# Reordering the start of a chunked linear recurrence: when input tiles are normalised, and which unit's levels go first

## The chip, the core and the metric

The kernel runs on one NeuronCore of one Trainium2 chip. The metric is the device time of one execution in microseconds (us), the median over several runs. The engines are named as in the profile: PE (matmuls; PEld is its weight loads), DVE (VectorE), ACT (ScalarE), POOL (GpSimd) and SP (the queue from which the DMAs are issued). Each engine works through its own queue in order.

## What is computed

One layer of a hybrid mixer over 2048 tokens of 1024 channels: RMS norm, one input projection that is split among three branches, an output projection, a second RMS norm and a residual. The branch that matters here is the first, a gated linear recurrence in four heads of 64 by 64 state:

```python
def step(S, inp):
    qi, ki, vi, gi = inp
    b = jnp.cumsum(gi, axis=2)
    decay = jnp.exp(jnp.where(causal, b_t - b_s, 0.0)) * causal_f
    attn = jnp.einsum('bhtd,bhsd,bhtsd->bhts', qi, ki, decay)
    o = einsum(attn, vi) + einsum(qi * jnp.exp(b), S)
    S = jnp.exp(b_last)[..., None] * S + einsum(ki * jnp.exp(b_last - b), vi)
    return S, o
```

The other two branches, a trailing-window mean and a causal attention with forget gates in eight heads, come after it in the program and are not touched.

## The kernel before, in words

**Input tiles.** The 2048 tokens are 16 tiles of 128, tile 0 to tile 15. `x_parts` (lines 205 to 223) prepares one tile in steps: a load of 512 KB (`xt`, SP), the square with its row sum (`xh`, `ss`, ACT L213), a small sum (DVE L214), a power (POOL L217), the scaled high half (`xh`, ACT L218), the low half (`xl`, DVE L220), and two transposing DMAs into `hTh` and `hTl` (SP L221, L223). Loads go into two `xt` buffers, so a tile's load can be issued when the tile two before it has been read for the last time, by its L220.

**Units.** The recurrence is worked in eight units, four groups `g` of 512 tokens by two channel blocks `ct`: unit 0 is (g 0, ct 0), unit 1 is (0, 1), unit 2 is (1, 0). A name such as `b_1_0` carries g and ct. A unit has three parts:

- features, `hgrn_f` (line 247) and `hgrn_q`: a projection on PE (`pf`, `pq`), then a chain over ACT, DVE and POOL: `E` and `z` (L254 to L257), `sg` (L260), `E` again (L265 to L269), the running sum `b` (L271), `nb` (L274), the factors `Kd` and `Qd` (L281 to L283, L308), `khat`, `qhat` (L286 to L289, L309), `el` (L291), and `qs` from the second projection (L301 to L307);
- levels, `hgrn_unit` (line 315): first matmuls `pd` with the mask `at` (L327, L329) and the transposed keys `khT` (PE L333, ACT L335); then for six block sizes h = 64, 32, 16, 8, 4, 2 a tile `X` (POOL L348, L349, ACT L350), two halves of `Z` (DVE L355), the matmul `pl` (PE L359) and a masked copy into `at` (DVE L363). After the second level the state moves on: `pu` from `khT` (PE L368) and eight updates of `S` (DVE L378). After the fourth, `po` is begun from those states (PE L383);
- the end: `po` is finished (PE L391), squared (ACT L394), summed (DVE L396, L397), raised to a power (POOL L398), scaled to `ma` (DVE L400) and stored.

**What sets the order.** The Python code is the program order. A scheduler then lays the instructions of every engine out, with program order as the priority. An edit of the code's order therefore moves instructions on all engines. In the first part of the program (`ordered`) the given order is kept.

**Around the change.** Tiles 0 to 5 are prepared for the first projections. Before unit 0's levels, tiles 6 and 7 are prepared and tiles 8 and 9 loaded ahead. From then on `feed` (line 596) yields three steps a tile, and every level of a unit takes one step (`next(xfeed, None)`, line 385), so that tiles 8 and 9 are prepared behind unit 0's six levels, 10 and 11 behind unit 1's, and so on. For each unit the loop then works through the next unit's features, the end of the unit before, and this unit's levels, with other projections (`pi`, `pk`) between the levels. Unit 0 has an order of its own (`if n == 0`).

Of the kernel before, what the change touches and what calls it, by code (L numbers as in the profile page):

```python
# [23 lines left out]
NT = T // P  # L24
# [19 lines left out]
GCPRE = 8  # L44
RATE = 0.45
POOL_LV = (64, 32, 16, 8, 4, 2)
LOGP = math.log(256.0)
NEG = -1e30

# [5 lines left out]
def kernel(  # L55
# [144 lines left out]
    def x_dma(xpool, t, tag="xt"):  # L200
        xt = (xpool if tag == "xt" else ap).tile([P, D], F32, tag=tag, name=f"xt{t}", bufs=2)
        sp(nc.sync.dma_start(xt, xf[t * P:(t + 1) * P, :]))
        xts[t] = xt
# [21 lines left out]
    def x_load(xpool, t, tag="xt"):  # L225
        for _ in x_parts(xpool, t, tag):
            pass
# [20 lines left out]
    def hgrn_f(g, ct, wf, bank=None):  # L248
        u = f"_{g}_{ct}"
        pf = (bank or pj)(f"pf{u}")  # L250
        proj_cm(pf, wf, ct * P, g)
        yield
        z, E = tmp(f"z{u}"), tmp(f"E{u}")
        S.activation(E, pf, AF.Abs, bias=0.0, scale=INV)  # L254
        S.activation(z, pf, AF.Copy, bias=0.0, scale=INV)
        S.activation(E, E, AF.Exp, bias=0.0, scale=-1.0)
        S.activation(E, E, AF.Ln, bias=1.0, scale=1.0)  # L257
        sg = tmp(f"sg{u}")

        V.scalar_tensor_tensor(sg, z, 0.0, E, op0=ALU.min, op1=ALU.subtract)  # L260
        E1 = V if g == 0 else G
        E1.tensor_tensor(z, sg, z, op=ALU.subtract)
        lk = lbt[:, 8 + ct:9 + ct]

        V.tensor_scalar(E, sg, -43.0, None, op0=ALU.max)  # L265
        S.activation(E, E, AF.Exp, bias=0.0, scale=-1.0)
        S.activation(E, E, AF.Ln, bias=lbt[:, 4 + ct:5 + ct], scale=lbt[:, 2 + ct:3 + ct])
        V.tensor_tensor(E, E, sg, op=ALU.add)
        V.tensor_scalar(E, E, lbt[:, 6 + ct:7 + ct], None, op0=ALU.max)  # L269
        b = t512("b", f"b{u}")  # L270
        V.tensor_tensor_scan(b, d0, E, initial=0.0, op0=ALU.mult, op1=ALU.add)  # L271

        nb = t512("nb", f"nb{u}")
        V.scalar_tensor_tensor(nb, z, lk, b, op0=ALU.add, op1=ALU.subtract)  # L274

        lfo = sg
        E1.tensor_tensor(lfo.rearrange("p (n two) -> p n two", two=2),
                        E.rearrange("p (n two) -> p n two", two=2),
                        odd.unsqueeze(1).to_broadcast([P, GT // 2, 2]), op=ALU.mult)
        q_d, k_d = t512("Qd", f"Qd{u}"), t512("Kd", f"Kd{u}")  # L280
        E1.tensor_tensor(k_d, z, lfo, op=ALU.subtract)  # L281
        S.activation(k_d, k_d, AF.Exp, bias=lk, scale=1.0)
        S.activation(q_d, lfo, AF.Exp, bias=0.0, scale=1.0)  # L283
        kk = t512("khat", f"khat{u}")
        bt = b.rearrange("p (n t) -> p n t", t=P)
        G.tensor_tensor(kk.rearrange("p (n t) -> p n t", t=P), bt[:, :, P - 1:P].to_broadcast([P, 4, P]), nb.rearrange("p (n t) -> p n t", t=P), op=ALU.add)  # L286
        S.activation(kk, kk, AF.Exp, bias=0.0, scale=1.0)
        e = t512("qhat", f"qhat{u}")
        S.activation(e, b, AF.Exp, bias=0.0, scale=1.0)  # L289
        el = ap.tile([P, 4], F32, tag="el", name=f"el{u}", bufs=2)  # L290
        V.tensor_copy(el, e.rearrange("p (n t) -> p n t", t=P)[:, :, P - 1])  # L291
        feats[(g, ct)] = dict(nb=nb, b=b, qd=q_d, kd=k_d, kk=kk, qh=e, el=el)
# [19 lines left out]
    def run(steps):  # L312
        for _ in steps:
            pass

    def hgrn_unit(g, ct, va):
        f = feats.pop((g, ct))
        nb, b, qs = f["nb"], f["b"], f["qs"]
# [19 lines left out]
        for li, h in enumerate(LEVELS):  # L338
            X = t512("X", f"X{u}_{h}", 4)
            Z = Zs[zc[0] % NZ]  # L340
            zc[0] += 1
            bv = b.rearrange("p (n two h) -> p n two h", two=2, h=h)
            nbv = nb.rearrange("p (n two h) -> p n two h", two=2, h=h)
            Xv = X.rearrange("p (n two h) -> p n two h", two=2, h=h)
            n = GT // (2 * h)
            mid = bv[:, :, 0, h - 1:h].to_broadcast([P, n, h])
            E1 = G if h in POOL_LV else V
            E1.tensor_tensor(Xv[:, :, 1, :], bv[:, :, 1, :], mid, op=ALU.subtract)  # L348
            E1.tensor_tensor(Xv[:, :, 0, :], mid, nbv[:, :, 0, :], op=ALU.add)  # L349
            S.activation(X, X, AF.Exp, bias=0.0, scale=1.0)  # L350
            qv = qs.rearrange("p (t n two h) -> p t n two h", t=4, two=2, h=h)
            X5 = X.rearrange("p (t n two h) -> p t n two h", t=4, two=2, h=h)
            for hh in range(2):
                r = slice(64 * hh, 64 * hh + 64)
                V.tensor_tensor(Z[r, :, hh, :].rearrange("p t (n h) -> p t n h", h=h), X5[r, :, :, 1, :], qv[r, :, :, 1, :], op=ALU.mult)  # L355
            pl = pm(f"pl{u}_{h}")
            plv = pl.rearrange("p (t u c) -> p t u c", t=4, u=2)
            for tt in range(4):
                PE.matmul(plv[:, tt].rearrange("p u c -> p (u c)"), X[:, tt * P:(tt + 1) * P], Z[:, tt].rearrange("p u c -> p (u c)"),  # L359
                          start=tt == 0, stop=tt == 3, skip_group_check=True)  # L360
            n2 = 64 // h
            dst = at.rearrange("p t u (n two h) -> p (t u) n two h", two=2, h=h)[:, :, :, 1, :]
            V.copy_predicated(dst, masks[h].rearrange("p (n h) -> p n h", h=h).unsqueeze(1).to_broadcast([P, 8, n2, h]),  # L363
                              pl.rearrange("p (u n h) -> p u n h", u=8, h=h))
            if li == 1:
                pu = pm(f"pu{u}")
                for tt in range(4):
                    PE.matmul(pu[:, tt * P:(tt + 1) * P], khT[:, tt * P:(tt + 1) * P], va[:, tt, ct * P:(ct + 1) * P],  # L368
                              start=tt == 0, stop=tt == 3, skip_group_check=True)
                olds = []  # L370
                for tt in range(4):
                    old = Sst[ct][Scur[ct] % NS]
                    Scur[ct] += 1
                    new = Sst[ct][Scur[ct] % NS]
                    olds.append(old)
                    for hh in range(2):
                        r = slice(64 * hh, 64 * hh + 64)
                        V.scalar_tensor_tensor(new[r, r], old[r, r], f["el"][r, tt:tt + 1],  # L378
                                               pu[r, tt * P + 64 * hh:tt * P + 64 * hh + 64], op0=ALU.mult, op1=ALU.add)
            if li == 3:  # L380
                po = pm(f"po{u}")
                for tt in range(4):
                    PE.matmul(po[:, tt * P:(tt + 1) * P], f["qh"][:, tt * P:(tt + 1) * P], olds[tt], start=tt == 0, stop=False,  # L383
                              skip_group_check=True)
            next(xfeed, None)
            if li % 2 == 1:
                yield "L"
        for tt in range(4):
# [69 lines left out]
    xpool = xstk.enter_context(tc.tile_pool(name="xpool", bufs=2, side="right", reuse_waits="tile"))  # L458
# [32 lines left out]
    wf, load, halves = w_parts([(FA, 256)], "f")  # L491
# [41 lines left out]
    wq = load_w([(QA, 256)], "q")  # L533
# [11 lines left out]
    for h in LEVELS:  # L545
# [4 lines left out]
                        fill=0, base=0, channel_multiplier=1)  # L550
        G.affine_select(out=m, in_=m, pattern=[[2 * h, nb], [0, h]], compare_op=ALU.is_ge,
                        fill=0, base=h - 1, channel_multiplier=-1)
# [35 lines left out]

    run(hgrn_q(0, 0, wq))
    wk0 = load_w([(KCOL, 256)], "k0", pool=gwp)  # L590
    x_load(xpool, 6)
    x_dma(xpool, 8)
    x_load(xpool, 7)
    x_dma(xpool, 9)

    def feed():

        for t in range(8, NT):
            parts = x_parts(xpool, t)
            for k in range(3):  # L600
                next(parts)
                if k < 2:
                    yield
            next(parts, None)
            if t + 2 < NT:
                x_dma(xpool, t + 2)
            yield

    xfeed = feed()
    prev = None  # L610
    kq = None
    for n, (g, ct) in enumerate(units):
# [24 lines left out]
        if n == 0:  # L637
            fs, qs = hgrn_f(0, 1, wf, pm), hgrn_q(0, 1, wq)
            next(fs)
            next(qs)  # L640
            toks[1] = new_tokens(1)
            tok_i(4, wi, toks[1])
            tok_i(5, wi, toks[1])
            next(gen)
            next(gen)
            run(fs)
            run(qs)
            fill(0)
            next(gen)
            fill(1)  # L650
            fill(2)
            fill(3)
            next(gen)
            prev = gen
            continue
# [547 lines left out]
```

## Time and profile before

| | us |
|---|---|
| median of 3 runs | 1248.82 (1247.8 to 1250.89) |
| the profiled execution's own time | 1248.18 |
| its span, first to last instruction | 1246.4 |
| PE busy | 1170.5 (94% of the span) |
| DVE busy | 812.2 (65%) |
| ACT busy | 609.5 (49%) |
| POOL busy | 403.7 (32%) |

How to read it: the busy shares are over the whole span. The recurrence with its features takes about the first fifth; what follows it are projections, attention and the output projection. The clock of PE is given as the share of its full speed that was granted, 1.00 for 2.4 GHz and 0.5 for 1.2 GHz; a stretch between the two has had both.

### The profile page before, as it was taken

Reading aid. Unit: us, or ns where it says so; the run is one execution under the profiler, and the core shown is the slowest. Engines: PE = TensorE matmul, PEld = TensorE weight load, DVE = VectorE, ACT = ScalarE, POOL = GpSimd, SP = SyncE. Lnnn points to the kernel's source line nnn. Section 1 sums busy time; section 2 is a strip of 40 time slices with the busy share of each in tenths; the row PEclk is TensorE's granted clock in tenths of the full one; section 3 lists DMA queues with packets and bytes.
Section 4 is the critical chain, followed back from the end, with each engine's and each line's share of the span. In section 5 each row is a group of like instructions: output and inputs, shape, how many; then the busy total and the mean of one; then the engine's idle time right before and its main releaser. Section 6 shows DMA issues by size and latency. Waiting matters only on the chain.

```text
span 1246.4 us, 25487 instructions
## 1 busy us (share of the span) xinstructions
PE 1170.5 (94%) x9949; PEld 749.9 (60%) x9949; DVE 812.2 (65%) x1736; ACT 609.5 (49%) x1176; POOL 403.7 (32%) x500
## 2 busy tenths in 40 slices
PE   5877999999999999999999999999989899999998
PEld 3445667655644588884447767755555555555544
DVE  5787878887433243214364799788788888888522
ACT  5756444553121222212122677667767676777611
POOL 2645555553130020002230223234334343434400
PEclk9988999999999999999999999999999999999999
DMA  9646100113175232101112343285223222321263
GB/s 226 184 115 170 44 17 18 52 35 93 43 183 142 71 107 71 35 2 43 26 51 70 89 140 110 69 178 127 67 64 85 68 78 79 65 51 38 80 162 104
DMA packets 168137, 107.56 MB, mean 86 GB/s; under 512 B 95824, under 2 KB 159568, under 8 KB 168016
## 3 DMA queue, kind: packets, MB, share of 16 engines
q1 hardware_dynamic: 166976, 105.92, 32.2%
q8 instruction: 78, 1.28, 0.4%
q14 instruction: 43, 0.35, 0.1%
q10 hardware_dynamic: 1040, 0.00, 0.0%
HBM read 59.62 MB, written 31.59 MB: 73 GB/s over the span
## 4 chain that ended last, share of the span: by engine, by line
PE 62%; DVE 19%; ACT 6%; issue 5%; POOL 4%; DMA 4%; SPq 0%; POOLq 0%; DVEq 0%; ACTq 0%
PE y L1078 11%; PE pq L183 7%; PE pv L194 6%; PE pgc L194 5%; PE pu L183 3%; PE st L1009 3%; PE st L1010 3%; PE pgb L183 3%; PE pk L183 3%; DVE pl L1024 3%; PE mx L973 3%; DVE M L979 3%; PE o L1034 2%; PE o L1035 2%; PE pf L183 2%
## 5 line engine op out<-in xcount | busy, mean ns | idle before, releaser
L1019 ACT ACTIVATE pf<-st,biasg 128x512 f32<-128x512 f32 (+1 forms) x320 | 199.6, 625 | 93.9 <-PE st L1010 53.2
L194 PEld LDWEIGHTS <-hTh 128*128 128x128 f16 x1536 | 151.0, 99 | 44.3 <-DMA hTh<-xh 16.1
L1024 DVE TENSOR_TENSOR pl<-pf,ph 128x512 f16<-128x512 f32 (+1 forms) x213 | 139.9, 658 | 42.4 <-POOL ph L1021 24.8
L1024 POOL TENSOR_TENSOR pl<-pf,ph 128x512 f16<-128x512 f32 (+2 forms) x107 | 114.2, 1067 | 147.7 <-ACT ph L1023 137.6
L979 DVE TENSOR_REDUCE M<-mx 128x1 f32<-128x512 f32 x192 | 129.2, 682 | 9.4 <-PE mx L973 8.5
L1023 ACT ACTIVATE ph<-st,biasg 128x512 f16<-128x512 f32 (+2 forms) x213 | 131.4, 617 | 2.1 <-PE o L1036 2.1
L1034 PE MATMUL o<-Vt,ph 128*128 128x65 f16 x1088 | 129.7, 193 | 2.8 <-DVE oc L1048 2.4
L1035 PE MATMUL o<-Vt,ph 128*128 128x64 f16 x1088 | 130.2, 195 | 0.0
L1036 PE MATMUL o<-Vt,pl 128*128 128x65 f16 x1088 | 129.2, 192 | 0.0
L1021 POOL TENSOR_SCALAR ph<-pf 128x512 f16<-128x512 f32 (+1 forms) x107 | 66.0, 617 | 192.4 <-ACT pf L1019 130.8
L1034 PEld LDWEIGHTS <-ph 128*128 128x128 f16 x1088 | 102.6, 96 | 34.5 <-issue 5.5
L1009 PE MATMUL st<-QQ,K 128*128 128x512 f16 (+1 forms) x320 | 111.5, 349 | 5.6 <-ACT ph L1023 5.0
L1035 PEld LDWEIGHTS <-ph 128*128 128x128 f16 x1088 | 101.8, 97 | 24.5 <-issue 1.1
L1036 PEld LDWEIGHTS <-pl 128*128 128x128 f16 x1088 | 102.3, 99 | 0.4
L1078 PE MATMUL y<-woh,mh 128*128 128x512 f16 (+2 forms) x264 | 98.2, 373 | 0.0
L1078 PE MATMUL y<-woh,ml 128*128 128x512 f16 (+2 forms) x264 | 98.0, 373 | 0.0
L1078 PE MATMUL y<-wol,mh 128*128 128x512 f16 (+2 forms) x264 | 98.0, 373 | 0.0
L973 PE MATMUL mx<-KA,QM 68*128 68x512 f16 (+1 forms) x224 | 79.5, 358 | 5.7 <-DVE M L979 4.1
L194 PEld LDWEIGHTS <-hTl 128*128 128x128 f16 x768 | 75.5, 98 | 9.9
L1010 PE MATMUL st<-QB,KA 68*128 68x512 f16 x224 | 80.1, 358 | 0.0
L1078 PEld LDWEIGHTS <-mh 128*128 128x128 f16 x528 | 49.4, 98 | 50.4 <-issue 0.7
L976 DVE CUSTOM_DVE_ANT_0 mx<-mx,negq 128x128 f32<-128x128 f32 (+3 forms) x128 | 62.3, 492 | 12.0 <-PE mx L973 11.5
(327 smaller groups left out, 2691.1 us busy)
## 6 DMA issues: line engine op xcount, KB each, us to landing
xt<-in_x_dram SPq DMA_DIRECT2D x16, 512.0 KB, 4.4
xr<-in_x_dram SPq DMA_DIRECT2D x16, 512.0 KB, 4.5
out_dram<-yt SPq DMA_DIRECT2D x15, 512.0 KB, 3.1
QQ<-qh_d SPq DMA_DIRECT2D x64, 64.0 KB, 2.3
wo<-in_w_out_dram SPq DMA_DIRECT2D x16, 256.0 KB, 3.0
gc_d<-gtc SPq DMA_DIRECT2D x32, 128.0 KB, 2.0
gtl<-gc_d SPq DMA_DIRECT2D x16, 256.0 KB, 2.9
wst_q<-in_w_in_dram SPq DMA_DIRECT2D x12, 256.0 KB, 2.9
```

The costliest lines, as they stand in the source:

```text
L183: PE.matmul(ps, a[:, k, c0:c0 + P], b[:, k, :], start=i == 0, stop=i == 3 * KC - 1)
L194: PE.matmul(ps, a[:, k, :], b[:, k, c0:c0 + n], start=i == 0, stop=i == 3 * KC - 1)
L979: V.tensor_reduce(dst, mx[:, :w], op=ALU.max, axis=AX.X)
L1009: PE.matmul(st[:, off:], K2[c][:, h, jj * P:(jj + 1) * P], QQs[i][:, off:], start=True, stop=False)
L1010: PE.matmul(st[:, off:], KA[c][:68, h, jj * P:(jj + 1) * P], QBs[i][:68, off:], start=False, stop=not diag)
L1019: S.activation(pf[:, off:], st[:, off:], AF.Exp, bias=bias, scale=0.125)
L1023: S.activation(ph[:, off:], st[:, off:], AF.Exp, bias=bias, scale=0.125)
L1024: (G if k == 1 else V).tensor_tensor(pl[:, off:], pf[:, off:], ph[:, off:], op=ALU.subtract)
L1034: PE.matmul(pov[:, qi, :], ph[:, qs], Vt[:, j, h, 0:65], start=(j == 0 and qi == 0), stop=False, skip_group_check=True)
L1035: PE.matmul(pov[:, qi, 0:64], ph[:, qs], Vt[:, j, h, 65:129], start=False, stop=False, skip_group_check=True)
L1036: PE.matmul(pov[:, qi, :], pl[:, qs], Vt[:, j, h, 0:65], start=False, stop=(j == 4 * g + qi), skip_group_check=True)
L1078: PE.matmul(py, a[:, k, :], b[:, k, cs], start=i == 0, stop=i == 3 * KC - 1)
```

## The change

Three edits. First, tiles 6 and 7 are no longer prepared before unit 0: only their loads are issued there, and `feed` begins with tile 6. A table FEED says how many steps each level takes: in unit 0 one, one, one, two, two, two, in unit 1 the other way round, in units 2 and 3 one each, none later. So tiles 6 to 8 belong to unit 0, 9 to 11 to unit 1, and from tile 12 on the units are those of before. Second, the first step of `hgrn_f` now includes the two ACT instructions that empty the projection's PSUM bank. Third, unit 1 (`n == 1`) gets an order of its own: only the two projections of unit 2's features, with the emptying of the first, go ahead of unit 1's levels; the rest of `hgrn_f` comes behind the first two levels and the rest of `hgrn_q` behind the next two. No arithmetic is changed, and the number of instructions is the same.

```diff
+FEED = ((1, 1, 1, 2, 2, 2), (2, 2, 2, 1, 1, 1), (1,) * 6, (1,) * 6) + ((0,) * 6,) * 4
...
         proj_cm(pf, wf, ct * P, g)
-        yield
         z, E = tmp(f"z{u}"), tmp(f"E{u}")
         S.activation(E, pf, AF.Abs, bias=0.0, scale=INV)
         S.activation(z, pf, AF.Copy, bias=0.0, scale=INV)
+        yield
...
-            next(xfeed, None)
+            for _ in range(FEED[2 * g + ct][li]):
+                next(xfeed)
...
-    x_load(xpool, 6)
-    x_dma(xpool, 8)
-    x_load(xpool, 7)
-    x_dma(xpool, 9)
+    x_dma(xpool, 6)
+    x_dma(xpool, 7)
...
-        for t in range(8, NT):
+        for t in range(6, NT):
...
+        if n == 1:
+
+            fs, qs = hgrn_f(nxt[0], nxt[1], wf), hgrn_q(nxt[0], nxt[1], wq)
+            next(fs)
+            next(prev)
+            next(qs)
+            next(gen)
+            fill(0)
+            fill(1)
+            next(gen)
+            run(fs)
+            fill(2)
+            next(gen)
+            run(qs)
             fill(3)
             next(gen)
             prev = gen
+            continue
```

What the scheduler makes of it is seen in the built order of each engine. The line numbers of the changed kernel are two or three higher than those of before (L213 is L215, L220 is L222, L271 is L273, L335 is L337, L355 is L357). Three places follow.

The first place is ACT's queue ahead of `khT`, the transposed keys of unit 0. Before:

```order
L266 ACTIVATE E_0_1_774<-E_0_1_774 128x512
L304 ACTIVATE th_0_1_804<-th_0_1_804 128x512
L213 ACTIVATE xh7_593,ss7_592<-xt7_590 128x1024
L213 ACTIVATE xh8_742,ss8_741<-xt8_588 128x1024
L218 ACTIVATE xh7_593<-xt7_590,ss7_592 128x1024
L239 ACTIVATE va1_654<-pi5_682 128x256
L240 ACTIVATE fcs_72<-pi5_682 128x8
L335 ACTIVATE khT_0_0_727<-pk_0_0_722 128x512
```

Now:

```order
L220 ACTIVATE xh7_855<-xt7_578,ss7_854 128x1024
L268 ACTIVATE E_0_1_606<-E_0_1_606 128x512
L306 ACTIVATE th_0_1_780<-th_0_1_780 128x512
L241 ACTIVATE va1_634<-pi5_662 128x256
L242 ACTIVATE fcs_72<-pi5_662 128x8
L269 ACTIVATE E_0_1_606<-E_0_1_606,lbt_324 128x512
L307 ACTIVATE th_0_1_780<-th_0_1_780 128x512
L215 ACTIVATE xh8_910,ss8_909<-xt8_835 128x1024
L337 ACTIVATE khT_0_0_707<-pk_0_0_702 128x512
```

The squares of tile 7 and its high half have moved forward. The square of tile 8 still stands ahead of `khT`, but tile 8's load is now issued after tile 6 is done instead of ahead of all.

The second place is DVE from the gate's running sum `b` of unit 2 to the second half of `Z` of unit 1's level 8, for which PE waits. Before:

```order
L274 SCALAR_TENSOR_TENSOR nb_1_0_986<-z_1_0_970,lbt_324,b_1_0_984 128x512
L291 COPY el_1_0_999<-qhat_1_0_997 128x4
L214 TENSOR_SCALAR ss13_1527<-ss13_1527 128x1
L307 TENSOR_TENSOR qs_1_0_1048<-th_1_0_1043,pq_1_0_1018 128x512
L220 SCALAR_TENSOR_TENSOR xl13_1529<-xt13_1238,ss13_1527,xh13_1528 128x1024
L214 TENSOR_SCALAR ss14_1760<-ss14_1760 128x1
L363 COPY_PREDICATED at_0_1_1052<-m64_397,pl_0_1_64_1132 128x8x64
L355 TENSOR_TENSOR Z0_454<-X_0_1_8_1187,qs_0_1_809 64x4x64
L363 COPY_PREDICATED at_0_1_1052<-m32_401,pl_0_1_32_1149 128x16x32
L355 TENSOR_TENSOR Z0_454<-X_0_1_8_1187,qs_0_1_809 64x4x64
```

Now:

```order
L222 SCALAR_TENSOR_TENSOR xl12_1436<-xt12_1176,ss12_1434,xh12_1435 128x1024
L273 SCALAR_TENSOR_TENSOR b_1_0_1142<-d0_391,E_1_0_959 128x512
L309 TENSOR_TENSOR qs_1_0_1205<-th_1_0_1200,pq_1_0_979 128x512
L276 SCALAR_TENSOR_TENSOR nb_1_0_1144<-z_1_0_958,lbt_324,b_1_0_1142 128x512
L216 TENSOR_SCALAR ss13_1527<-ss13_1527 128x1
L293 COPY el_1_0_1157<-qhat_1_0_1155 128x4
L365 COPY_PREDICATED at_0_1_1004<-m64_397,pl_0_1_64_1084 128x8x64
L357 TENSOR_TENSOR Z0_454<-X_0_1_8_1178,qs_0_1_785 64x4x64
L365 COPY_PREDICATED at_0_1_1004<-m32_401,pl_0_1_32_1103 128x16x32
L357 TENSOR_TENSOR Z0_454<-X_0_1_8_1178,qs_0_1_785 64x4x64
```

The low half of tile 13 no longer stands ahead of these `Z`; it comes behind unit 2's first three levels of `Z`.

The third place is DVE in the features of unit 3, from `ma` to the running sum. Before:

```order
L400 TENSOR_TENSOR ma_0_1_1310<-po_0_1_1199,rs_0_1_1306 128x512
L268 TENSOR_TENSOR E_1_1_1266<-E_1_1_1266,sg_1_1_1271 128x512
L269 TENSOR_SCALAR E_1_1_1266<-E_1_1_1266,lbt_324 128x512
L303 TENSOR_SCALAR th_1_1_1338<-th_1_1_1338 128x512
L271 SCALAR_TENSOR_TENSOR b_1_1_1279<-d0_391,E_1_1_1266 128x512
```

Now:

```order
L403 TENSOR_TENSOR ma_0_1_1310<-po_0_1_1190,rs_0_1_1306 128x512
L216 TENSOR_SCALAR ss15_1855<-ss15_1855 128x1
L270 TENSOR_TENSOR E_1_1_1266<-E_1_1_1266,sg_1_1_1271 128x512
L271 TENSOR_SCALAR E_1_1_1266<-E_1_1_1266,lbt_324 128x512
L222 SCALAR_TENSOR_TENSOR xl15_1857<-xt15_1588,ss15_1855,xh15_1856 128x1024
L273 SCALAR_TENSOR_TENSOR b_1_1_1279<-d0_391,E_1_1_1266 128x512
```

Tile 15's low half has moved from ahead of these features, where it stood before, into their middle.

## Rows read from the trace of the kernel before

**Rows 1.** The page's 40 slices of 31.2 us: PE and its granted clock

```profile
PE   5877999999999999999999999999989899999998
...
PEclk9988999999999999999999999999999999999999
```

**Rows 2.** Windows: PE, PEld, DVE, ACT, POOL busy us (x instructions), clock, DMA share, GB/s

```profile
60.00:160.00 100.00, 81.77 (x554) 58.84 (x553) 80.52 (x139) 56.51 (x103) 55.91 (x58) 0.90 0.43 106
160.00:1246.00 1086.00, 1047.23 (x9162) 666.60 (x9159) 692.04 (x1515) 514.05 (x999) 319.54 (x381) 1.00 0.29 78
```

**Rows 3.** Timeline of PE: start, us, instruction, [idle before <- releaser]

```profile
71.31 2.08 PE L368 MATMUL pu<-va,khT 128*128 128x128 f32 x8 [6.55 <-ACT khT L335]
...
87.34 1.13 PE L359 MATMUL pl<-Z,X 128*128 128x128 f32 x8 [1.83 <-DVE Z L355]
...
122.75 2.05 PE L359 MATMUL pl<-Z,X 128*128 128x128 f32 x8 [7.78 <-DVE Z L355]
...
126.29 2.94 PE L183 MATMUL pf<-hTh,wh_f 128*128 128x512 f16 x8
...
151.71 1.16 PE L368 MATMUL pu<-va,khT 128*128 128x128 f32 x8 [1.46 <-ACT khT L335]
...
160.78 1.95 PE L359 MATMUL pl<-Z,X 128*128 128x128 f32 x16
162.56 1.89 PE L183 MATMUL pf<-hTh,wh_f 128*128 128x512 f16 x8
```

**Rows 4.** Timeline of DVE before unit 0's state update and after it

```profile
59.05 1.69 DVE L220 SCALAR_TENSOR_TENSOR xl<-xt,ss,xh 128x1024 f16<-128x1024 f32 x1
60.66 3.70 DVE L355 TENSOR_TENSOR Z<-X,qs 64x256 f32<-64x256 f32 x6
...
75.68 2.16 DVE L378 SCALAR_TENSOR_TENSOR S<-S,el,pu 64x64 f32<-64x64 f32 x7
77.88 0.69 DVE L268 TENSOR_TENSOR E<-E,sg 128x512 f32<-128x512 f32 x1
...
79.20 0.48 DVE L269 TENSOR_SCALAR E<-E,lbt 128x512 f32<-128x512 f32 x1
...
79.93 1.21 DVE L271 TENSOR_TENSOR_SCAN b<-d,E 128x512 f32<-128x512 f32 x1
```

**Rows 5.** Tile loads: issue (SP), square that waited (ACT), all 16; ACT's khT

```profile
77.99 0.59 SPq L202 DMA_DIRECT2D xt<-in_x_dram  x1
...
82.23 1.06 ACT L213 ACTIVATE xh<-xt 128x1024 bf16<-128x1024 f32 x1 [1.08 <-DMA xt<-in_x_dram]
...
DMA to landing us min/median/max: 3.8/4.4/5.6
...
70.67 0.59 ACT L335 ACTIVATE khT<-pk 128x512 f32<-128x512 f32 x1
```

**Rows 6.** Windows of DVE alone: busy us, clock, DMA share, GB/s

```profile
77.84:122.60 44.76, 35.10 (x57) 0.95 0.57 146
122.60:151.26 28.66, 22.62 (x39) 0.90 0.27 64
```

**Rows 7.** Timeline of DVE at unit 1's levels and at unit 2's

```profile
118.52 1.28 DVE L220 SCALAR_TENSOR_TENSOR xl<-xt,ss,xh 128x1024 f16<-128x1024 f32 x1 [1.20 <-ACT xh L218]
119.72 0.15 DVE L214 TENSOR_SCALAR ss<-ss 128x1 f32<-128x1 f32 x1
...
121.85 0.75 DVE L355 TENSOR_TENSOR Z<-X,qs 64x256 f32<-64x256 f32 x1
...
160.07 1.30 DVE L355 TENSOR_TENSOR Z<-X,qs 64x256 f32<-64x256 f32 x3
```

**Rows 8.** Timeline of DVE and POOL at unit 3's running sum

```profile
145.70 2.06 DVE L271 TENSOR_TENSOR_SCAN b<-d,E 128x512 f32<-128x512 f32 x1
...
145.60 1.09 POOL L277 TENSOR_TENSOR sg<-E,odd 128x512 f32<-128x512 f32 x1 [1.99 <-DVE E L269]
146.76 2.07 POOL L281 TENSOR_TENSOR Kd<-z,sg 128x512 f32<-128x512 f32 x1
```

More of the change, by code (lines that the diff above doesn't have):

```diff
@@ L651 @@
             fill(2)
+            fill(3)
+            next(gen)
+            prev = gen
+            continue
[10 more added lines that the diff above has]
+            fill(2)
+            next(gen)
+            run(qs)
             fill(3)
```

## The prediction

> **What bounds the kernel now.** I read the page's slices first. PE is near 9 tenths from the sixth slice on, at full clock, and lower before [rows 1]. The windows make that sharp: from 160 us to the end PE is busy 1047.23 of 1086 us, and from 60 to 160 only 81.77 of 100, at a granted clock of 0.90 [rows 2]. So the last 1086 us are PE's, and what happens before 160 counts only by when PE gets there: a microsecond won or lost at 160 is one at the end. DVE is not full in that stretch either (80.52 of 100): it is a chain, not a load, that holds PE.
>
> The timeline of PE names the links [rows 3]. PE waits 6.55 us for `khT` of unit 0, 1.83 for `Z` of unit 0's level 8, 7.78 for `Z` of unit 1's level 8, 1.46 for `khT` of unit 2. After the two long waits the clock is at its lower level (1.2 GHz) for a while: eight `pf` matmuls take 2.94 us at 126.29 and 1.89 at 162.56, eight `pl` 2.05 at 122.75 and 1.13 at 87.34, which is 2.0 us in these two rows. After the wait of 1.83 it stayed up. From 160 on no wait of this kind is left.
>
> **The change, part by part.** The work is the same, so only places in queues count. I follow the DVE queue, since most links end there, past three stations.
>
> Station A, `khT` of unit 0. Ahead of the first `Z`, DVE had tile 6's low half (1.69) and now has two more weight halves, about as long, so `Z` starts at 60.66 as before [rows 4]. Four `Z` instead of six follow (3.70 / 6 = 0.62 each), then tile 6's low half (1.28, a row of 118.52 without POOL beside it, rows 7): it ends at 60.66 + 2.47 + 1.28 = 64.4. Only then can SP send tile 6's low transpose (1.23) and tile 8's load, at 65.6. One such load was issued at 77.99 and its square began at 82.23, so 4.2 us; all 16 landed within 3.8 to 5.6 [rows 5]. I take 4.2, the row with the same neighbours. The square begins at 69.9, ends 1.1 us later, `khT` stands right behind it and takes 0.59, and `pu` starts at 71.7 instead of 71.31 [rows 3]. The longest wait of PE therefore stays, 0.4 us longer: one tile's square leaves ACT's queue there, and a load comes into it. The low clock after it stays too.
>
> Station B, `Z` of unit 1's level 8, which ended at 121.85 + 0.75 = 122.6 [rows 7]. The state updates come first. They ended at 75.68 + 2.16 = 77.84, held up by the low halves of tiles 7 and 8. Now they need only `pu` (71.7 + 2.08 = 73.8) and a queue that, walked through in the same way, is done by 74.0, so they take 2.4 us to 76.4: 1.4 earlier. In front of them now stand `E`, `E` and `b` of unit 1, 0.69 + 0.48 + 1.21 = 2.4 us that came behind before [rows 4]. From the updates to station B, DVE was busy 35.10 us of 44.76, so it waited 9.7 [rows 6]. That stretch loses the 2.4 us, loses tile 13's 1.28 + 0.15 [rows 7], and gains tile 8's 1.28. Its waits shift: tile 13's wait (1.20) goes; new ones come for tile 10's and tile 11's squares, whose loads also follow a low half now. Walked through with the durations of the rows, the waits come out half a microsecond longer. Sum: -1.4 - 2.4 - 1.4 + 1.3 + 0.5 = -3.4, so `Z` ends near 119.2, and PE's long wait of 7.78 shrinks by that. It is still some 5 us, and I leave the low clock as it is.
>
> Station C, DVE from there to unit 2's levels. Before, 22.62 busy of 28.66: 6.0 of waits [rows 6]. Now tile 13 is in it (+1.4), the waits for the high halves of tiles 14 and 15 stand at other places and cost 0.7 more in the walk, and tile 15's low half lies beside POOL's work, where such an instruction took 1.69 instead of 1.28 [rows 4, 7] (+0.4). The lead falls to -3.4 + 2.5 = -0.9. PE is better off for a moment: `khT` of unit 2 now stands right behind `Kd`, ahead of four ACT instructions that it followed, and its wait of 1.46 goes. But PE then runs up to DVE. Before, the last `Z` of level 2 was ready at 160.07 + 0.42 = 160.5 and its `pl` began at 160.78 + 0.9 = 161.7, so PE had 1.2 us in hand there [rows 3, 7]. That slack and the lead of 0.9 are what PE can gain: 2.1, rounded to 2.0. What is late next is PE itself, from 162 on.
>
> That tile 15's low half shares its time with POOL is worth a second look. At 145.70 `b` took 2.06 us; alone it took 1.21 [rows 4]. It began while POOL's `sg` ran until 146.69 and ended 1.07 after that; POOL's `Kd` began at 146.76, and ended 1.07 after `b` [rows 8]. They took turns. The Trainium skill, SBUF — State Buffer, section Who interferes with whom, says so as a rule: a DVE instruction with two SBUF inputs and a GpSimd instruction that reads SBUF hold the shared ports one after the other, each for its whole length. It speaks against this change: tile 15's low half would be one more turn of 1.28 against `sg` and `Kd`, and by the rule the gain would be 1.1 instead of 2.0, as an estimate. I keep the 0.4 of the rows, since `b` would lose the turn that the low half takes.
>
> Other parts cost nothing. Emptying the projection's bank one step earlier moves two ACT instructions by at most 1 us, at places where the matmuls that want the bank wait for something else; were that cover gone, it would be a gain of the same size. The next weight loads now go out on SP ahead of tile 6's transposes; tile 6's low transpose waits for its low half anyway, and those weights are first used far later. Tiles 6 and 7 are transposed about 10 us after their old places at the latest, and PE first needs both for unit 2's projection, which stands behind all of unit 0's levels. From tile 12 on the feed is as before.
>
> Bounds: of the two loads on the chain (tiles 8 and 11), 3.8 to 5.6 instead of 4.2 each, -0.8 to +2.8 in all; the added waits of station C could be nothing, -1.1. That makes 1244.9 to 1249.6 for the forecast alone. The sum is made against the profiled execution's 1248.18, which becomes 1246.2; that execution is 0.64 below the median of 1248.82, for which I say 1246.8. About 0.3% (3.7 us) is what a measurement of this kernel can tell from no change.
>
> **The rivals.** *The lead survives* (faster). If tiles 13 and 15 fall into waits that DVE has anyway, station C keeps -3.4 or so, and PE gains 1.2 + 3.4 = 4.6, a little less where `khT` limits it: 1244.4. If the wait at unit 1 then gets so short that PE's clock does not fall, another 2.0 comes: 1242.4. For it: DVE waits 6.0 of 28.66 us in that stretch, room for 1.4. Against: those waits are themselves for ACT's halves of these tiles.
>
> *The loads become the chain* (slower). Before, the tiles' loads went out long ahead; now tile 8's square waits for a load just issued, with `khT` queued behind it on ACT, and tile 11's square stands ahead of unit 2's `E`. Each late microsecond counts at both. At 5.2 us a load nothing is left of the gain, beyond it the kernel is slower: 1249.6 at 5.6, and more where the transposes on the same queue hold a load up: I say 1250.5. For it: squares already waited for loads at 82.23 [rows 5]. Against: half of all loads landed within 4.4 us. The Trainium skill, DMA: Bandwidth & Descriptors, section Rules for kernel authors, tells one to issue a DMA early and wait for it late; the change does the opposite for tile 8, and the row of 82.23 agrees that such a load is felt.
>
> *It does not reach 160* (no change). If `Z` and the updates of unit 2 come at their old times, PE's shorter waits in units 1 and 2 turn into one at unit 2's level 8: 1248.8 within half a microsecond. The order does change on every engine, so that it does nothing at all is excluded.
>
> **How the numbers follow.** Forecast 0.45, lead survives 0.28, loads 0.19, no change 0.08. The forecast is within 0.3% in all but its edges (0.04 faster, 0.01 slower). The surviving lead is beyond it in 0.23 of its 0.28. The loads are slower by over 0.3% in 0.10 of 0.19. So faster 0.27, same 0.62, slower 0.11. The range goes from 1242.6, nearly all of the first rival, to 1251.6, past the second's usual end; some 0.15 is left out.
>
> **What would show it.** In the changed profile: `pu` of unit 0 at 71.5 to 72, after the square of tile 8; the state updates ending near 76.4; the `pl` of unit 1's level 8 near 119.3 with a wait of 5 to 6 us before it and the low clock behind it; `pu` of unit 2 some 4 us earlier than 151.71, with no wait; the first `pf` of unit 3 near 160.5 instead of 162.56; nothing else different after that. It is wrong if `pu` of unit 0 comes after 73.5 (the loads), or if that `pf` comes before 158.8 (the lead survives).

## The result, and the profile after

The changed kernel takes 1253.84 us (median of 10 executions, 1251.92 to 1255.45); the kernel before, on the same chip, 1250.87 (10 executions). The ratio is 1.0027, with a 95% interval of 1.0016 to 1.0037: 2.0 to 4.6 us slower. The forecast was 2.0 us faster, called no change, and 1253.84 lies beyond the range's upper end of 1251.6. The sign is that of the rival "the loads become the chain", which had 0.19. The forecast was counted from three executions of the kernel before (1248.82); its ten now give 1250.87. Counted from there the range would end at 1253.65, and the result would lie only just beyond it. The sign would be wrong all the same.

The windows of the changed kernel, as in [rows 2] (PE, PEld, DVE, ACT, POOL busy, clock, DMA share, GB/s):

```profile
60.00:160.00 100.00, 77.63 (x517) 55.12 (x515) 80.16 (x130) 54.47 (x96) 49.25 (x51) 0.90 0.49 111
160.00:1253.00 1093.00, 1054.55 (x9202) 672.96 (x9200) 696.19 (x1524) 516.40 (x1004) 325.02 (x388) 0.99 0.29 77
```

PE has 4.1 us less work behind it at 160 us than before (77.63 against 81.77). Its timeline tells where, to be read beside [rows 3]. The first line is a row that the change does not touch, the last block of unit 1's first projection; before, it stood at 47.98:

```profile
48.22 1.89 PE L185 MATMUL pf<-hTl,wh_f 128*128 128x512 f16 x8
...
72.89 2.07 PE L370 MATMUL pu<-va,khT 128*128 128x128 f32 x8 [8.68 <-ACT khT L337]
...
84.75 1.13 PE L361 MATMUL pl<-Z,X 128*128 128x128 f32 x8 [2.49 <-DVE Z L357]
...
124.64 2.05 PE L361 MATMUL pl<-Z,X 128*128 128x128 f32 x8 [8.21 <-DVE Z L357]
...
151.51 1.16 PE L370 MATMUL pu<-va,khT 128*128 128x128 f32 x8
155.59 0.38 PE L196 MATMUL pi<-wh_i,hTh 128*128 128x264 f16 x1 [2.92 <-ACT fcs L242]
...
167.00 1.89 PE L185 MATMUL pf<-hTh,wh_f 128*128 128x512 f16 x8
```

Every wait of [rows 3] but the last is longer (8.68 us for 6.55, 2.49 for 1.83, 8.21 for 7.78). The wait for `khT` of unit 2 is gone, as forecast, but a new one of 2.92 for the bank of `pi`, which ACT's `fcs` empties, stands 4 us behind it. The last row comes at 167.00 instead of 162.56, 4.44 later. (The prediction calls this `pf` unit 3's. It is unit 4's, of group 2; only the name was wrong.) The two profiled executions differ by 7.3 us, the medians by 3.0; the changed one's is the slowest of its ten, so nothing of its trace later than this row is used below.

From the untouched row to that `pf` it is 114.58 us before (47.98 to 162.56) and 118.78 now. I call this **the distance**. It leaves out how late a profiled execution got to that row (47.95 to 49.45 us in the runs). The loss to explain is 4.2 us of it.

Where it arises is read on DVE, by the prediction's stations. Station A: the timelines of DVE and POOL ahead of unit 1's gate (the chain `sg`, `z`, `E`, `b`), and behind it the one row of the kernel before that is needed beside them:

```profile
57.41 3.86 DVE L166 SCALAR_TENSOR_TENSOR wl_k<-wst_k,g,wh_k 128x256 f16<-128x256 f32 x4
61.19 1.73 DVE L357 TENSOR_TENSOR Z<-X,qs 64x256 f32<-64x256 f32 x4
62.95 1.28 DVE L222 SCALAR_TENSOR_TENSOR xl<-xt,ss,xh 128x1024 f16<-128x1024 f32 x1
64.16 1.81 DVE L357 TENSOR_TENSOR Z<-X,qs 64x256 f32<-64x256 f32 x2
66.00 0.99 DVE L262 SCALAR_TENSOR_TENSOR sg<-z,E 128x512 f32<-128x512 f32 x1
67.03 1.21 DVE L264 TENSOR_TENSOR z<-sg,z 128x512 f32<-128x512 f32 x1
68.16 0.41 DVE L267 TENSOR_SCALAR E<-sg 128x512 f32<-128x512 f32 x1
...
75.36 2.44 DVE L380 SCALAR_TENSOR_TENSOR S<-S,el,pu 64x64 f32<-64x64 f32 x8
...
63.45 1.38 POOL L350 TENSOR_TENSOR X<-b 128x256 f32<-128x256 f32 x1 [2.46 <-PE pl L361]
64.79 0.90 POOL L351 TENSOR_TENSOR X<-b,nb 128x256 f32<-128x256 f32 x1
65.65 0.80 POOL L350 TENSOR_TENSOR X<-b 128x256 f32<-128x256 f32 x1
66.41 1.28 POOL L351 TENSOR_TENSOR X<-b,nb 128x256 f32<-128x256 f32 x1
```

```profile
65.72 0.42 DVE L265 TENSOR_SCALAR E<-sg 128x512 f32<-128x512 f32 x1
```

`E` comes 19.94 us behind the untouched row (68.16 - 48.22), before 17.74 (65.72 - 47.98): 2.2 later. ACT waits for that `E`:

```profile
45.35 1.05 ACT L215 ACTIVATE xh<-xt 128x1024 bf16<-128x1024 f32 x1
...
68.61 0.63 ACT L268 ACTIVATE E<-E 128x512 f32<-128x512 f32 x1 [3.78 <-DVE E L267]
...
71.21 1.05 ACT L215 ACTIVATE xh<-xt 128x1024 bf16<-128x1024 f32 x1
...
72.25 0.59 ACT L337 ACTIVATE khT<-pk 128x512 f32<-128x512 f32 x1
```

The square of tile 8 (71.21) has no wait for its load, so the load is not what makes `khT` late. ACT stands still for `E`, 3.78 us. The row at 45.35 is tile 7's square, which now stands ahead of the weights' high halves on ACT.

Station B, DVE's windows from the state updates' end to the `Z` of unit 1's level 8, and from there to the first masked copy of unit 2's levels, as in [rows 6]:

```profile
77.80:124.50 46.70, 34.65 (x54) 0.97 0.57 130
124.50:155.67 31.17, 24.63 (x41) 0.94 0.36 77
```

The loads of tiles 10, 11 and 12 in it, by ACT's waits, then DVE's waits behind the first of them, then two DVE instructions that lay beside POOL's:

```profile
97.83 1.06 ACT L215 ACTIVATE xh<-xt 128x1024 bf16<-128x1024 f32 x1 [3.14 <-DMA xt<-in_x_dram]
102.19 1.06 ACT L215 ACTIVATE xh<-xt 128x1024 bf16<-128x1024 f32 x1 [0.98 <-DMA xt<-in_x_dram]
107.98 1.06 ACT L215 ACTIVATE xh<-xt 128x1024 bf16<-128x1024 f32 x1 [1.11 <-DMA xt<-in_x_dram]
...
99.02 0.15 DVE L216 TENSOR_SCALAR ss<-ss 128x1 f32<-128x1 f32 x1 [2.59 <-ACT xh L215]
101.25 1.28 DVE L222 SCALAR_TENSOR_TENSOR xl<-xt,ss,xh 128x1024 f16<-128x1024 f32 x1 [1.63 <-ACT xh L220]
...
81.33 1.76 DVE L310 TENSOR_TENSOR Qd<-Qd,qs 128x512 f32<-128x512 f32 x1
115.71 2.06 DVE L273 TENSOR_TENSOR_SCAN b<-d,E 128x512 f32<-128x512 f32 x1
```

### The profile page after: what moved, and what is told of

The parts are those of the page before. It is cut to its first block, busy times and chain, and to the rows that moved or that the text cites. A ratio compares the mean times of both kernels' runs of the same rounds, so it can differ in the third digit from the quotient of the medians.

```text
span 1253.7 us, 25481 instructions
## 1 busy us (share of the span) xinstructions
PE 1173.4 (94%) x9949; PEld 752.1 (60%) x9949; DVE 814.6 (65%) x1736; ACT 609.1 (49%) x1176; POOL 403.4 (32%) x500
## 3 DMA queue, kind: packets, MB, share of 16 engines
q8 instruction: 78, 1.28, 0.4%
## 4 chain that ended last, share of the span: by engine, by line
PE 63%; DVE 19%; ACT 5%; DMA 4%; issue 4%; POOL 4%; SPq 1%; POOLq 0%; DVEq 0%; ACTq 0%
PE y L1097 11%; PE pq L185 7%; PE pv L196 6%; PE pgc L196 5%; PE st L1028 3%; PE pu L185 3%; PE st L1029 3%; PE pk L185 3%; PE pgb L185 3%; PE mx L992 3%; DVE pl L1043 3%; DVE M L998 3%; PE pf L185 2%; PE o L1053 2%; PE o L1054 2%
```

## The experiments

All are told with the distance of their one profiled execution and the ratio of their time to the kernel before, run on the same chip. How much a distance varies from execution to execution was not measured:

| run | distance, us | against before | ratio (95% interval) |
|---|---|---|---|
| before | 114.58 | | 1 |
| the change | 118.78 | +4.2 | 1.0027 (1.0016 to 1.0037) |
| feed_alone | 115.81 | +1.2 | 1.0018 (1.0007 to 1.0029) |
| order_alone | 113.96 | -0.6 | 0.9990 (0.9979 to 1.0001) |
| tile15_behind | 118.52 | +3.9 | 1.0028 (1.0018 to 1.0038) |
| tile12_behind | 118.67 | +4.1 | 1.0038 (1.0025 to 1.0050) |
| no_load_10_11 | 118.22 | +3.6 | 1.0025 (1.0011 to 1.0038) |
| late_12_15 | 114.10 | -0.5 | 1.0069 (1.0054 to 1.0084) |
| late_12_15_unit1 | 108.41 | -6.2 | 1.0040 (1.0024 to 1.0055) |
| late_12_15_before | 109.83 | -4.8 | 1.0048 (1.0031 to 1.0066) |
| tile8_left_out | 117.13 | +2.6 | 1.0004 (0.9994 to 1.0014) |
| tile8_late | 114.24 | -0.3 | 1.0001 (0.9989 to 1.0013) |
| tiles_at_first_levels | 118.24 | +3.7 | 1.0048 (1.0036 to 1.0060) |
| tiles_12_15_spread | 109.10 | -5.5 | 1.0000 (0.9990 to 1.0010) |
| no_loads_from_8 | 115.28 | +0.7 | 1.0011 (1.0001 to 1.0022) |
| square7_behind | 116.05 | +1.5 | 1.0005 (0.9997 to 1.0014) |
| square7_no_loads | 113.03 | -1.6 | 1.0000 (0.9986 to 1.0014) |
| square7_14_15 | 114.15 | -0.4 | 1.0007 (0.9994 to 1.0020) |
| tiles_14_15_spread | 112.39 | -2.2 | 0.9978 (0.9967 to 0.9989) |

Where an expectation speaks of a distance, it counts from a row 2.8 us earlier: 121.6 there is 118.8 here. "Unit 3's pf" is again unit 4's.

**Half of the change each.** feed_alone takes back the second and third edit, order_alone the first. Of feed_alone, against the changed kernel:

```diff
+        yield
         z, E = tmp(f"z{u}"), tmp(f"E{u}")
         S.activation(E, pf, AF.Abs, bias=0.0, scale=INV)
         S.activation(z, pf, AF.Copy, bias=0.0, scale=INV)
-        yield
...
-        if n == 1:
...
```

> Before 1250.9, changed kernel 1253.8. Only the first edit: tiles 6 and 7 behind unit 0's levels, with FEED; unit 1 in the order of before. Theory 1 (only both edits together cost: they put tile 13 and tile 15 back among units 2's and 3's chains): no loss, 1249 to 1251, the first pf of unit 3 at 161 to 163 us. Theory 2 (the feed costs, by tile 8's and later loads that are issued late): 1253 to 1254, that pf at 166 to 167. Theory 3 (unit 1's order costs): 1249 to 1251 as well.

> Only the second and third edit: the bank emptied a step earlier, and unit 1's own order; the tiles as before. Theory 1: no loss, 1250 to 1251.5; the sums of unit 0's output now stand ahead of unit 2's gate, which may take a microsecond of the lead. Theory 2: 1250 to 1251. Theory 3: 1253 to 1254, with a new wait of 2 to 4 us of PE between 120 and 160 us.

Unit 1's order costs nothing by itself: theory 3 falls. The feed costs something alone, by time two thirds of the loss, by distance less than a third: theories 1 and 2 each hold in part. Together the halves cost 3.6 us of distance more than their sum (4.2 against 1.2 - 0.6).

**Single tiles moved behind the features they stood in.** `issue_after` queues an instruction behind another on its engine; `bins` holds each unit's running sum `b`, and PIN says which tile waits for which.

```diff
-                next(parts)
+                with tc.issue_after(bins[PIN[t]].ins) if t in PIN else ExitStack():
+                    next(parts)
...
+    PIN = {15: (1, 1)}
```

> The changed kernel with tile 15's sum and low half queued behind unit 3's running sum b on DVE; nothing else moves on DVE before it. Theory 1 with the loss in unit 3's features: b of unit 3 comes 1.5 to 2.5 us earlier, PE's wait of 2.9 us for pi falls under 1, the first pf of unit 3 is at 164 to 165 instead of 167, and the time at 1251 to 1252. If the loss was all made before (tiles 10 to 12 in unit 2's features): the wait only moves, pf at 166 to 167, 1253 to 1254.

In tile15_behind tile 15 stands behind `b` of unit 3, in tile12_behind tile 12 behind `b` of unit 2.

> The changed kernel with tile 12's sum and low half queued behind unit 2's running sum b on DVE. If the tiles in unit 2's features carry the loss: b of unit 2 1.3 to 2 us earlier than 115.7, Z of unit 1's level 8 at 122 to 123 instead of 123.7, PE's wait of 8.2 us a microsecond or more shorter, 1252 to 1253. If unit 3's features carry it: PE's wait shortens as well but comes back for pi, 1253.5 to 1254.5.

Neither gives anything back. PE's new wait for `pi` went with tile 15's place, but the loss did not. In tile15_behind PE waits here instead:

```profile
154.16 1.16 PE L371 MATMUL pu<-va,khT 128*128 128x128 f32 x8 [2.30 <-ACT khT L338]
```

The wait that one sees last is only where the lateness shows.

**All four late tiles out of the features.** Tiles 12 to 15 are fed behind unit 3's levels and queued behind `b` of unit 4, with the change, with unit 1's order alone, and with the kernel before:

```diff
-FEED = ((1, 1, 1, 2, 2, 2), (2, 2, 2, 1, 1, 1), (1,) * 6, (1,) * 6) + ((0,) * 6,) * 4
+FEED = ((1, 1, 1, 2, 2, 2), (2, 2, 2, 1, 1, 1), (0,) * 6, (2,) * 6) + ((0,) * 6,) * 4
...
+    PIN = {12: (2, 0), 13: (2, 0), 14: (2, 0), 15: (2, 0)}
```

> The changed kernel with tiles 12 to 15 fed behind unit 3's levels and queued on DVE behind the running sum b of unit 4, so none of them stands in the features of units 2 and 3. If the tiles' turns of square, power, high half and low half in that chain carry the loss: Z of unit 1's level 8 at about 122 instead of 123.7, the pf of 167.0 at 161 to 163, 1247.5 to 1250. If the loss lies elsewhere (order of unit 1, PE's bank for pi): pf at 165 or later, 1252 to 1254.

> The second and third edit alone, tiles 6 to 11 as before, tiles 12 to 15 fed late as in the run above. By the theory of the tiles in the chain DVE loses four low halves (5.1 us) and their waits ahead of the pf that stood at 161.9 with these edits alone: pf at 157 to 159, 1244.5 to 1247, faster than both kernels. If PE or ACT ends the stretch first: pf at 160.5 to 162, 1248 to 1250.

> The kernel before with tiles 12 to 15 fed late. By the same theory pf at 158 to 160 instead of 162.6, 1245.5 to 1248; if PE or ACT ends the stretch, 1249.5 to 1251.

The distance falls by 4.7, 5.6 and 4.8 us: 1.2 to 1.4 a tile, in all three alike. So a tile in that stretch costs about its low half (1.28), the prediction's price, and since the kernel before pays it too, it is not the loss. And the time got worse: PE pays behind 160 us, where the prediction saw nothing but PE. In late_12_15:

```profile
193.44 1.13 PE L362 MATMUL pl<-Z,X 128*128 128x128 f32 x8 [2.54 <-DVE Z L358]
...
202.09 2.05 PE L362 MATMUL pl<-Z,X 128*128 128x128 f32 x8 [5.07 <-DVE Z L358]
```

**Loads and tile 8.** In no_load_10_11 and no_loads_from_8 those tiles read the buffer's old data; in tile8_left_out its columns take tile 7's halves; in tile8_late, with the feed of before, its low half stands behind `el` of unit 1. Of no_loads_from_8:

```diff
+            xt = xts[t]
             parts = x_parts(xpool, t)
...
-                x_dma(xpool, t + 2)
+                xts[t + 2] = xt
```

> The changed kernel in which tiles 10 and 11 have no load of their own and take the data of tiles 8 and 9 that still lies in the buffers (so the input of these two is left out). Theory 1 (tile loads that are issued late push the whole stream of tiles back by a buffer's turn, and with it tiles 12 to 15 into the features of units 2 and 3): ACT's waits of 3.1 and 1.0 us for these loads go, tile 13 comes back ahead of unit 1's levels and tile 15 ahead of unit 3's features, the pf that stands at 167.0 us comes at 162 to 164.5, 1249.5 to 1251.5. Rival (the new order of unit 0 and POOL's turns against DVE carry it): pf at 166 or later, 1253 to 1254.

> The changed kernel in which tile 8 is not prepared: its columns take tile 7's halves, so its load, square, power and halves are left out. If the loss is that tile 8's turn moved from ahead of unit 0's state updates into the stretch behind them (the stream of tiles one turn behind): the pf that stands at 167.0 us comes at 163 to 164.5, Z of unit 1's level 8 at 121.5 to 122.5 instead of 123.7, 1250 to 1251.5. If it is the new order of unit 1's gate ahead of the state updates, with POOL's turns beside DVE: pf at 165.5 to 167, 1252.5 to 1254.

> The kernel with unit 1's order alone (1249.3, pf at 161.9) in which tile 8's low half is queued on DVE behind el of unit 1, some 12 us later, and nothing else of the feed is changed. If a late tile 8 carries the loss: the loads of tiles 10 and 11 come later, pf at 163.5 to 165, 1251 to 1252.5. If it does not: the state updates come 1.5 us earlier and pf at 160.5 to 162.5, 1248.5 to 1250.

Two loads less give back 0.6 us: ACT no longer waits for them, but DVE then waits elsewhere, for halves of tiles 11 and 12 among others. Leaving tile 8 out gives back 1.7 us of distance, little more than a tile costs anywhere (by its time more, 2.3 thousandths). And with the old feed, tile 8's low half could come 12 us later for 0.3 us more distance than in order_alone, with no change in time that is clear of noise. So neither tile 8's lateness nor these two loads are the cause.

**Tiles 6 to 8 at the first three levels.** FEED of unit 0 becomes (3, 3, 3, 0, 0, 0).

> The changed kernel with all nine steps of tiles 6 to 8 at unit 0's first three levels: on ACT khT stands ahead of tile 8's square, on DVE tile 8's low half comes some 5 us earlier and unit 1's b behind the state updates, as in the kernel before. If the late tile 8 carries the loss: pf at 164 to 166 instead of 167.0, 1251 to 1253. If unit 1's gate ahead of the updates carries it: pf at 163 or earlier, 1249.5 to 1250.5. If neither: 166.5 or later.

The distance stays (118.24) though tile 8 is earlier and `khT` ahead of its square. That left two things to try: tile 7's square, which stands ahead of unit 1's gate in the changed kernel, and late loads as a whole.

**Tile 7's square, and all loads.**

```diff
-                next(parts)
+                with tc.issue_after(bins["X", 0, 0, 8].ins) if t == 7 and k == 0 else ExitStack():
+                    next(parts)
```

> The changed kernel in which tiles 8 to 15 have no load (they take the data of tiles 6 and 7, so their input is left out); the order of DVE is the changed kernel's up to tile 9, and tiles 12 and 13 come earlier. Distance from the second pf of unit 1's first projection (45.4 us) to the pf at 167.0: 121.6 in the changed kernel, 117.4 before, 116.8 with unit 1's order alone. If late loads carry the loss: 117 to 118.5, 1249.5 to 1251. If the order ahead of them does (two weight halves of DVE that fell behind tile 7's square on ACT, POOL's turns): 120 or more, 1252.5 to 1254.

> The changed kernel with tile 7's square queued on ACT behind X of unit 0's level 8, as before; the weights' high halves come forward again, and with them two weight halves of DVE that had fallen behind 57 us. If DVE's later start ahead of unit 1's gate carries the loss: pu of unit 0 1.5 to 2 us nearer to the start (25.5 to 26.2 us behind that pf instead of 27.5), and the distance falls to 118.5 to 120, 1251 to 1252.5. If the tiles' lateness carries it, tile 7 and 8 being later still: 121 to 123, 1253.5 to 1255.

> Tile 7's square behind and no loads from tile 8 on, both together. Distance from the pf at 45.4 us to the pf at 167.0: changed kernel 121.6, square alone 118.9, no loads alone 118.1. If they are two costs side by side, both come back: 114.5 to 116, 1247 to 1249. If they are one cost that either takes away (ACT's queue ahead of DVE): 117.5 to 119, 1250.5 to 1252.

The square alone gives back 2.7 us of distance (118.78 to 116.05) and 2.2 thousandths of time, the loads 3.5 and 1.6 thousandths. Both together give 5.8 us, nearly the sum of 6.2, and 2.7 thousandths, less than the sum of 3.8. By distance they are two costs side by side. Together they are more than the loss of 4.2, since the kernel before waits for loads too [rows 5].

DVE's window from the untouched row to the first state update of unit 2 tells the two apart. In order: before, the change, feed_alone, square7_behind, no_loads_from_8, square7_no_loads (stretch, its length, DVE busy us and instructions, PE's clock, DMA share, GB/s):

```profile
47.98:154.41 106.43, 87.18 (x141) 0.90 0.43 107
48.22:158.81 110.59, 90.81 (x141) 0.91 0.46 103
49.25:157.47 108.22, 90.14 (x142) 0.92 0.46 105
48.70:157.16 108.46, 88.87 (x142) 0.91 0.44 105
49.19:156.75 107.56, 90.96 (x142) 0.90 0.28 67
49.45:154.75 105.30, 87.29 (x140) 0.92 0.30 68
```

The changed kernel's DVE reaches the update 4.2 us later. Of this 3.6 are busy time (90.81 against 87.18), and only 0.5 are waits (19.78 against 19.25). The kinds of instructions are the same but for one weight half more and one small sum less. The weight halves take 5.7 us instead of 4.0 (six instead of five), `el` 3.1 instead of 2.0, `Qd` 2.9 instead of 2.2; others, `b` and `nb` among them, take less. The square's run takes 1.9 us off the busy time. The loads' run takes 3.2 off the waits and nothing off the busy time. So DVE's waits, for loads or for other things, are nearly what they were: the loss is mostly DVE's busy time.

How the square works is read in square7_behind, DVE again:

```profile
58.32 1.64 DVE L166 SCALAR_TENSOR_TENSOR wl_k<-wst_k,g,wh_k 128x256 f16<-128x256 f32 x2
59.88 3.21 DVE L358 TENSOR_TENSOR Z<-X,qs 64x256 f32<-64x256 f32 x4
63.12 1.28 DVE L223 SCALAR_TENSOR_TENSOR xl<-xt,ss,xh 128x1024 f16<-128x1024 f32 x1
64.32 0.84 DVE L358 TENSOR_TENSOR Z<-X,qs 64x256 f32<-64x256 f32 x2
65.20 0.69 DVE L263 SCALAR_TENSOR_TENSOR sg<-z,E 128x512 f32<-128x512 f32 x1
65.93 0.69 DVE L265 TENSOR_TENSOR z<-sg,z 128x512 f32<-128x512 f32 x1
66.53 0.42 DVE L268 TENSOR_SCALAR E<-sg 128x512 f32<-128x512 f32 x1
```

Two weight halves stand ahead of `Z`, not four: 1.64 against 3.86 us. `E` comes 17.83 us behind the untouched row (48.70 there) instead of 19.94, 2.1 earlier. But the run does not isolate this. The state updates of unit 0 then end only 0.3 us earlier (29.32 us behind the row instead of 29.58), and the move re-laid more than those two halves: tile 13's low half came back ahead of unit 1's level 8, tile 15's ahead of unit 3's features, and 13 matmuls of unit 3's `pf` ran on PE ahead of level 8. And feed_alone has `E` as late (19.95) and loses 1.2 us. Shown is what the square's place costs, and that it costs DVE busy time; how much of it comes by `E` is not.

**Versions that could pay.** tiles_12_15_spread puts tiles 12 and 13 behind the `Z` of unit 3's level 16, where DVE had waited 4.4 us, and 14 and 15 behind the first `Z` of unit 4; tiles_14_15_spread only 14 and 15, at the first of these places; both with the old feed of tiles 6 to 11 and unit 1's order. square7_14_15 is the whole change with tile 7's square and tiles 14 and 15 so placed.

> Unit 1's order alone, with tiles 12 and 13 queued on DVE behind the Z of unit 3's level 16, where DVE waited 4.4 us for unit 4's gate, and tiles 14 and 15 behind the first Z of unit 4. The features of units 2 and 3 are then free of tiles, as in the run with late tiles: pf at 157 to 158.5, and if the waits of 2.5 and 5.1 us near 190 and 197 stay away, 1244 to 1246.5. If they come back in unit 4: 1248 to 1252.

> Unit 1's order alone, with only tiles 14 and 15 moved, behind the Z of unit 3's level 16, where DVE waited 4.4 us; their loads have long landed there. By 1.0 to 1.1 us a tile, which the runs with late tiles gave, pf at 159.5 to 160 instead of 161.9, and if ACT has no load to wait for, no new wait behind: 1246.5 to 1248.5. If the two tiles hold unit 4's gate up as in the run with four: 1249 to 1251.

> The changed kernel with tile 7's square behind and tiles 14 and 15 behind the Z of unit 3's level 16: distance 118.9 less 1.6, which the two tiles gave with unit 1's order alone: 117 to 117.8, 1249.5 to 1251; no faster than the run with unit 1's order and these two tiles (1248.9). If the whole change helps once these places are mended: below 1248.5.

Four tiles save 4.9 us of distance against order_alone and lose it again behind 160 (PE then waits 2.98 for `khT` of unit 3). Two tiles save 1.6 and keep it: 0.9978 of the kernel before, the only run that is faster beyond its interval (1248.87 us; the change, 1253.84). The whole change with both places mended comes back to the kernel before, no further: tiles 6 and 7 behind unit 0's levels bring nothing that was seen.

## Why the prediction was wrong

- **What bounds the kernel**: half right. PE reached the same place 4.44 us later, and the time followed (2.0 to 4.6). But DVE still matters behind 160 when work is moved there (late_12_15); "from 160 on no wait of this kind is left" held only for the order of before.
- **The step that failed is the lead at unit 1's level 8.** The `Z` there was forecast 3.4 us earlier than before, at 119.2. It ended at 124.5, 1.9 later. The 5.3 between them are 1.4 from station A, 2.0 of busy time and 1.9 of waits in station B. Behind most of it stands the premise "the work is the same, so only places in queues count": a place also sets what an instruction lies beside, and how long it takes. For this the sum had 0.4 us, in station C. Measured are 3.6 us more of DVE's busy time up to unit 2's updates, of a loss of 4.2.
- **Station A.** Forecast: `pu` at 71.7, held by tile 8's load, and updates that end at 76.4. Measured: 72.89 and 77.80. I followed `khT` by that load, which was not waited for, and not by `E`, for which ACT stands still first. The swap of tile 6's low half for two weight halves holds for the first `Z` (61.19 against 60.66). Ahead of unit 1's gate it is no swap: the low half still comes there, between the `Z`, and the two weight halves are added (2.2 us). POOL's `X` now run beside `sg` and `z`, which take 0.99 and 1.21 us (0.69 each in square7_behind), 0.8 more. The rest of that stretch gives 0.8 back, so `E` is 2.2 later. The halves fell there because tile 7's square moved ahead of them on ACT, and the prediction does not price that square's move. Its place costs 2.7 us in the end (square7_behind), by `E` and by what else moved with it.
- **Station B.** From the updates to that `Z` the forecast was 42.8 us, the window shows 46.70. Of the 3.9, 2.0 are busy time (34.65 against 32.6): the moved instructions left as forecast, but `Qd`, two `el` and the `b` of unit 2 took 1.8 us more than before, beside POOL. 1.9 are waits (12.05 against 10.2), mostly tile 10's (2.59 and 1.63 above). For it and tile 11 together I had added half a microsecond. (Against before, the waits are 2.4 more here and 2.4 fewer ahead of the updates' end, 1.14 instead of 3.50.)
- **Station C was right**: 31.17 us instead of 28.66, +2.5 as forecast. (Tile 13's low half is in it: it stands at 136.29, behind unit 1's last `Z`, not behind unit 2's first levels.) The turns of DVE and POOL, too: unit 3's `b` took 1.21 instead of 2.06, and tile 15's low half ahead of it took the turn (2.37). But the lead it started from was -1.9 instead of 3.4, so DVE came 1.9 + 2.5 = 4.4 later. By the prediction's own sum PE should have lost less, since it had 1.2 in hand there. It lost all 4.4: behind the new wait for `pi` its clock was at the lower level (granted 0.50), and 15 matmuls began 0.22 us apart instead of 0.11, 1.7 us in all:

```profile
155.77 0.42 PE L196 MATMUL pi<-wl_i,hTh 128*128 128x264 f16 x1
155.99 0.42 PE L196 MATMUL pi<-wh_i,hTl 128*128 128x264 f16 x1
...
162.63 0.28 PE L196 MATMUL pi<-wl_i,hTh 128*128 128x264 f16 x1
162.75 0.28 PE L196 MATMUL pi<-wh_i,hTl 128*128 128x264 f16 x1
...
155.60:158.70 3.10, 3.10 (x15) 0.50 0.00 0
```

- **The rivals**: "the loads become the chain" had the sign, but not the mechanism of the loss. Late loads do cost (3.5 us, no_loads_from_8), but DVE's waits are nearly what they were before (19.78 against 19.25). Tile 8's square, which it named first, did not wait; the squares of tiles 10, 11 and 12 did, and taking the loads of 10 and 11 away gave back 0.6. The Trainium skill, DMA: Bandwidth & Descriptors, section Rules for kernel authors, has the rule to issue a load early and wait for it late; ACT's three waits of 3.14, 0.98 and 1.11 us agree with it.
- **Open**: why the feed costs 3.6 us of distance more with unit 1's order than without. In feed_alone DVE is busy 3.0 us longer than before, nearly as much as with the change, but waits 1.2 less (18.08 against 19.25). PE there had other matmuls for the wait at unit 1's level 8, which was 3.67 us instead of 8.21; that this is all of it was not tried.

## What to carry to other kernels

Walk through a moved step on every queue from its first instruction on: here the new place of a square of one microsecond, hoisted on ACT ahead of weight halves, cost 2.7 us, more than the whole gain that was forecast. A stage with waits on PE can still be nearly full on the engine behind it (DVE 80 of 100 us here); there a step moved out of the way must land in a real gap, and the gap must be looked for behind the bound stage too. When a wait goes and the time stays, look upstream for the place where the chain became late, with an untouched row as the zero, and split the engine's time from that row into busy time and waits: if the busy time of the same instructions grew, no load and no wait explains it.

## What was not expected of the hardware

Even a tiny DVE instruction took several times as long beside POOL: the 128x4 copy `el` took 0.16 us in square7_behind and 1.01 in the changed kernel at the same step (78.65 and 79.09). Two `Z` took 0.84 and 1.81 (64.32 and 64.16 above):

```profile
78.65 0.16 DVE L294 COPY el<-qhat 128x4 f32<-128x4 f32 x1
```

```profile
79.09 1.01 DVE L293 COPY el<-qhat 128x4 f32<-128x4 f32 x1
...
78.65 1.43 POOL L288 TENSOR_TENSOR khat<-b,nb 128x512 f32<-128x512 f32 x1 [10.96 <-DVE nb L276]
```

In the changed kernel POOL's `khat` ran from 78.65 to 80.08, and `el` ended with it; in square7_behind POOL was idle there.
